# A list schedule, made in the source, sets the order of every engine of a hybrid encoder layer

## The chip, the cores and the metric

The kernel runs on one core of a Trainium2 chip. The core has TensorE (PE in the profile), VectorE (DVE), ScalarE (ACT), GpSimd (POOL) and SyncE (SP); each runs its own stream of instructions in order. SP issues nearly all transfers here, POOL a few. The metric is device microseconds of one execution.

## The reference

One layer of a streaming encoder, for 2048 prompt rows and for 8 running streams of 16 rows each that attend to 1024 cached rows. All matrices are float32.

```
h = rms_norm(x, norm_g)
z = einsum("btd,de->bte", h, w_in)                 # 1024 -> 3584 columns
u_a, v_a, g_a, q, k, v, g_b = split(z)             # 512 columns each
y_a = u_a * (tril(W_s) @ rms_norm(v_a) + b_s) * silu(g_a)      # in chunks of 128 rows
q, k = rms_norm(q), rms_norm(k)                    # per 64 columns
s = q @ k.T / 8 - slope * |distance|, masked by chunks of 64
o = (softmax(s_1) - lam * softmax(s_2)) @ v        # 4 heads, two halves each
y_b = rms_norm(o) * (1 - lam_init) * silu(g_b)
y = x + concat(y_a, y_b) @ w_out
```

The new keys, values and gate rows are outputs too.

## The kernel before, in words

Every float32 operand of a matmul is split into a high part, which ACT writes by a cast, and a low part, which DVE or POOL writes by a subtraction (`split`); a product is then two or three matmuls (`mm3`). Projection, the values of the prompt and the output projection take three.

The work is written as generators, each step of which emits a few instructions and yields its time on TensorE:

- Input projection and branch A (`stream` in `p1_pools`): 14 blocks of weight columns for the first 8 prompt tiles and the sample tile, then 14 for the other 8 tiles. A block's weights come in eight chunks (`load_w`: transfer to `wraw`, ACT and DVE split them into `w`); two row tiles share one accumulator (`acc`). Tiles of x are transposed on TensorE (`x_tp`, to `xT`). `mix` is the spatial gate.
- Sample attention (`sample_scores`, `sample_values`): `sk_tp` transposes cached keys, `sS` are scores, `sO` the products with values. Values come by SP into two buffers `svraw`, then ACT and POOL split them into two buffers `sv`.
- Prompt attention (`attention`): per head and pair of query tiles, `k_tp` and `q_tp` transpose keys and queries, `S` are scores, `a_tp` transposes of the probabilities, `oT` products with values, `o_tp` the transposes of a finished pair. Stage A does rows 0 to 1023 beside the second half of the projection, stage B the other rows beside the output projection.
- Output projection (`out_stream`): `y_tp` transposes rows of y (cast to `yT`), `oo` multiplies them by `wo`, the split `w_out`, whose raw chunks come into `woraw`.

`weave(a, b, ratio, ahead)` puts two generators together: it emits steps of `b`, and between them as many steps of `a` as `ratio` asks for. With `tc.issue_after` it also ties each step of `a` to a TensorE instruction of `b` some `ahead` steps back, so that `a` doesn't run too far ahead. The tile framework then orders the instructions of each engine: an instruction written earlier comes first, unless by the framework's own estimate of times it isn't ready and a later one is. SBUF pools lie over one another: when stage A's pools close, `wo` takes the space of the right side, and stage B's attention that of the projection on the left side.

## Time and profile before

| what | value |
|---|---|
| median of 3 runs | 1415.4 us (1412.22 to 1416.99) |
| span of the profiled execution | 1410.9 us |
| time of the profiled execution beyond its span | not in the page |
| TensorE busy | 1360.5 us, 96% |
| VectorE, ScalarE, GpSimd busy | 897.1, 794.0, 617.6 us |
| bytes moved | 183.06 MB, mean 130 GB/s |

Busy time of TensorE is the time in which at least one matmul is in flight. A window row shows, for a stretch of the span, each engine's busy time and instruction count, then TensorE's granted clock, the share of the 16 transfer engines in use, and GB/s. A wait row reads: engine, tile and line that waited, what released it, us in total, times, longest.

### The profile page before, as it was taken

What the parts mean: (1) busy time and instruction counts of PE and PEld (TensorE: products, weight loads), DVE (VectorE), ACT (ScalarE), POOL (GpSimd) and SP (SyncE); (2) the same over time, 40 slices, a digit from 0 to 9 for tenths busy, and PEclk for the clock granted to TensorE, in tenths of its full rate; (3) what the DMA queues carried; (4) which work ended last, traced back from release to release, by engine and by line L of the source; (5) the groups of instructions that cost most, each with busy time, mean ns of one, the idle gap of its engine ahead of it and who ended that gap; (6) DMA issues with size and microseconds to landing.
All of it is one profiled execution on the core that took longest, in us unless ns stands there. A gap on an engine that the chain in (4) does not pass through costs nothing.

```text
span 1410.9 us, 27990 instructions
## 1 busy us (share of the span) xinstructions
PE 1360.5 (96%) x9892; PEld 1266.1 (90%) x9892; DVE 897.1 (64%) x2114; ACT 794.0 (56%) x1778; POOL 617.6 (44%) x796
## 2 busy tenths in 40 slices
PE   7999999999999989899999999988999999999998
PEld 6999999999999979899999999986888888888887
DVE  5442366767565764786766767444888778878632
ACT  5442356666655775565554655443777767667520
POOL 2361535555554655656232331243555545444310
PEclk9999999999999999999999999998999999999999
DMA  7533244545444476445343332166555433433223
GB/s 220 175 91 100 78 122 124 169 130 158 130 140 145 142 220 203 112 112 138 96 128 83 99 96 69 42 211 207 149 158 162 142 115 117 143 97 94 75 94 101
DMA packets 209245, 183.06 MB, mean 130 GB/s; under 512 B 21104, under 2 KB 167024, under 8 KB 209104
## 3 DMA queue, kind: packets, MB, share of 16 engines
q1 hardware_dynamic: 199280, 155.17, 36.9%
q0 software_dynamic: 9824, 26.09, 6.8%
q8 instruction: 78, 1.28, 0.4%
q14 instruction: 63, 0.52, 0.1%
HBM read 130.86 MB, written 42.47 MB: 123 GB/s over the span
## 4 chain that ended last, share of the span: by engine, by line
PE 50%; DMA 7%; DVE 5%; ACT 3%; issue 3%; POOL 3%; SPq 1%; ACTq 0%; DVEq 0%; POOLq 0%
PE acc L73 16%; PE oo L73 12%; PE S L73 8%; PE oT L73 7%; PE a_tp L77 4%; DMA wraw<-in_w_in_dram 2%; DMA svraw<-in_cache_v_dram 1%; DMA woraw<-in_w_out_dram 1%; DVE ex L584 1%; DMA x<-in_x_prompt_dram 1%; DVE ex L568 1%; PE y_tp L77 1%; DMA qraw<-q_scr 1%; POOL sv L139 1%; DVE w L306 1%
## 5 line engine op out<-in xcount | busy, mean ns | idle before, releaser
L73 PE MATMUL acc<-w,xT 128*128 128x256 f32 x5376 | 719.4, 284 | 2.5 <-DVE w L306 0.9
L73 PEld LDWEIGHTS acc<-w,xT 128*128 128x128 f32 x5376 | 676.2, 190 | 14.8 <-issue 2.7
L73 PE MATMUL oo<-wo,yT 128*128 128x512 f32 x816 | 223.6, 405 | 6.6 <-ACT yT L138 6.6
L73 PE MATMUL S<-kT,qT 128*128 128x512 f32 (+3 forms) x688 | 185.8, 367 | 6.2 <-DVE sst L568 3.9
L572 ACT ACTIVATE ex<-ex,sst 128x128 f32<-128x128 f32 (+15 forms) x128 | 153.9, 1203 | 61.0 <-DVE sst L568 59.5
L73 PEld LDWEIGHTS oo<-wo,yT 128*128 128x128 f32 x816 | 148.9, 191 | 34.7 <-ACT yT L138 7.6
L306 DVE SCALAR_TENSOR_TENSOR w<-wraw,normg,w 128x256 fp32r<-128x256 f32 x224 | 119.6, 555 | 87.1 <-ACT w L305 79.1
L305 ACT ACTIVATE w<-wraw,normg 128x256 fp32r<-128x256 f32 x220 | 105.8, 505 | 87.8 <-DMA wraw<-in_w_in_dram 75.3
L73 PE MATMUL oT<-aT,v 128*128 128x256 f32 x864 | 151.8, 290 | 2.9 <-ACT aT L138 1.9
L568 DVE CUSTOM_DVE_ANT_0 ex<-S,dist,sst 128x512 f32<-128x512 f32 (+2 forms) x192 | 123.2, 652 | 37.6 <-PE S L73 35.8
L73 PEld LDWEIGHTS oT<-aT,v 128*128 128x128 f32 x864 | 124.3, 189 | 14.5 <-DVE aT L139 3.9
L139 POOL TENSOR_TENSOR sv<-svraw,sv 128x512 fp32r<-128x512 f32 (+1 forms) x72 | 96.6, 1346 | 75.5 <-ACT sv L138 59.1
L73 PEld LDWEIGHTS S<-kT,qT 128*128 128x128 f32 x688 | 110.4, 191 | 21.3 <-DVE sst L568 8.6
L138 ACT CAST aT<-a_tp 128x512 fp32r<-128x512 f32 (+1 forms) x144 | 79.3, 559 | 70.4 <-PE a_tp L77 68.5
L139 DVE TENSOR_TENSOR aT<-a_tp,aT 128x512 fp32r<-128x512 f32 (+1 forms) x144 | 94.3, 658 | 38.2 <-ACT aT L138 37.3
L568 DVE CUSTOM_DVE_ANT_0 ex<-S,dist 128x512 f32<-128x512 f32 (+3 forms) x128 | 79.6, 629 | 29.8 <-PE S L73 16.6
L77 PE MATMUL a_tp<-ident,ex 128*128 128x128 f32 x544 | 83.1, 273 | 4.3 <-DVE ex L584 3.3
L784 POOL TENSOR_TENSOR slo<-slo,dist_s 64x256 f32<-64x256 f32 (+1 forms) x64 | 49.4, 772 | 63.3 <-ACT slo L783 60.5
L139 POOL TENSOR_TENSOR v<-vraw,v 128x512 fp32r<-128x512 f32 x36 | 48.2, 1338 | 54.5 <-ACT v L138 45.4
L77 PEld LDWEIGHTS a_tp<-ident,ex 128*128 128x128 f32 x544 | 63.3, 140 | 8.5 <-DVE gbt L641 1.9
L584 DVE SCALAR_TENSOR_TENSOR ex<-ex,sst 128x1024 f32<-128x1024 f32 (+4 forms) x64 | 65.1, 1038 | 1.1
L588 POOL TENSOR_TENSOR ex<-ex 128x1024 f32<-128x1024 f32 (+4 forms) x32 | 58.4, 1848 | 15.9 <-ACT ex L587 11.4
(144 smaller groups left out, 1925.5 us busy)
## 6 DMA issues: line engine op xcount, KB each, us to landing
wraw<-in_w_in_dram SPq DMA_DIRECT2D x160, 128.0 KB, 2.5
skraw<-in_cache_k_dram SPq DMA_DIRECT2D x64, 256.0 KB, 3.1
svraw<-in_cache_v_dram SPq DMA_DIRECT2D x64, 256.0 KB, 2.9
kT<-k_scr POOLq DMA_DIRECT2D x20, 512.0 KB, 4.6
vraw<-out_dram SPq DMA_DIRECT2D x36, 256.0 KB, 2.8
y<-y_scr SPq DMA_DIRECT2D x34, 256.0 KB, 3.0
out_dram<-xo SPq DMA_DIRECT2D x34, 256.0 KB, 2.1
wraw<-in_w_in_dram SPq DMA_DIRECT2D x128, 64.0 KB, 2.2
```

Source lines behind the costliest of these rows:

```text
L73: pe.last = nc.tensor.matmul(*a, **k).ins
L77: pe.last = nc.tensor.transpose(*a, **k).ins
L138: act.copy(hi, src)
L139: (lo_eng or dve).tensor_tensor(out=lo, in0=src, in1=f(hi), op=ALU.subtract)
L305: act.activation(w[:, 0], r, AF.Copy, scale=normg[:, kc:kc + 1])
L306: dve.scalar_tensor_tensor(out=w[:, 1], in0=r, scalar=normg[:, kc:kc + 1], in1=f(w[:, 0]), op0=ALU.mult, op1=ALU.subtract)
L568: dve.tensor_tensor_reduce(out=ex[c][:, a:b], in0=s, in1=dist[:, off + a:off + b], scale=SLOPES[h], scalar=prev[c], op0=ALU.add, op1=ALU.m ...
L572: act.activation(ex[c][:, :w], ex[c][:, :w], AF.Exp, bias=prev[c], scale=-1.0, accum_out=st[:, c, 6:7])
L584: dve.scalar_tensor_tensor(out=p0, in0=p1, scalar=st[:, 1, 7:8], in1=p0, op0=ALU.mult, op1=ALU.add)
L588: pool.tensor_tensor(out=p0, in0=p1, in1=p0, op=ALU.add)
L784: pool.tensor_tensor(out=lo, in0=lo, in1=dist_s[rh, x:x + w_], op=ALU.add)
```

## The change

The order of all instructions is set in the source. When the whole program is written, and before the framework orders it, `Order(tc).run()` goes through the instruction list. It finds what each instruction must wait for from the memory that it reads and writes, which buffer of its tag each tile can take, and which tiles of a later pool lie over those of an earlier one. Then it plays a list schedule: each engine takes, whenever it is free, the first in program order of the instructions that are ready by then. Durations come from a table in `cost`; a transfer takes 1500 ns and its bytes at 280 per ns through one shared channel. An instruction on TensorE counts as ready only 150 ns (`SLACK`) after its producer on another engine has reached it, and one that waits for a transfer 150 ns (`LOAD`) after. The resulting order of each engine, SP and POOL with their transfers included, is handed to the framework as a chain of dependencies. In `weave` the tie with `tc.issue_after` is gone; the ratios and buffer counts are the same. The operations, their sizes, their buffers and the engine of each are the same; only comments are taken out besides, so a line n of the kernel before stands at about n + 288 in the code that follows the new class (L73 and L77 are now L361 and L365).

```diff
+class Order:
+    SLACK, LOAD = 150.0, 150.0
...
+    def cost(self, n):
+        kind = type(n.ins).__name__[4:]
+        size = max([math.prod([k for s, k in a.ap[1:]]) for a in n.reads + n.writes] or [1])
+        accum = len(n.writes) > 1
+        if n.dma:
+            return 0.0, 560.0 if n.engine == self.POOL else 400.0
+        if n.engine == self.PE:
+            size = math.prod([k for s, k in n.writes[0].ap[1:]])
+            t = 109.0 if size <= P else 4 + 0.4455 * size
+            return t + 165, t
+        if n.engine == self.ACT:
+            t = 165 + 0.83 * size if kind == "TensorCopy" else 205 + 0.835 * size
+            return (t + 180, t + 90) if accum else (t, t - 105)
+        if n.engine == self.DVE:
+            t = {"TensorTensor": 160 + 1.04 * size, "TensorReduce": 160 + 1.03 * size, "Memset": 100 + 0.5 * size,
+                 "Reciprocal": 162.0}.get(kind, 205 + 1.04 * size)
+            if kind == "TensorScalarPtr" and not n.ins.is_scalar_tensor_tensor:
+                t = 170 + 0.56 * size
+            return (t + 100, t - 40) if accum else (t, t - 85)
+        if kind == "Memset":
+            return 100 + 0.83 * size, 100 + 0.83 * size
+        if "pow" in str(n.ins):
+            return 300 + 200.0 * size, 250 + 200.0 * size
+        t = 190 + 2.16 * size if kind == "TensorTensor" else 195 + 1.1 * size
+        return t, t - 50
+    def run(self):
+        N = self.nodes
+        reach = {self.PE: 54.0, self.POOL: 80.0, self.SP: 27.0}
+        for n in N:
+            n.wait = len(n.deps)
+            for d in n.deps:
+                N[d].after.append(n.idx)
+        first = [[] for _ in N]
+        gate = [[] for _ in N]
+        def behind(a, b):
+            first[a].append(b)
+            N[b].wait += 1
+        for q in self.queue.values():
+            for a, b in zip(q, q[1:]):
+                if self.uses[a][0] != self.uses[b][0]:
+                    behind(self.uses[a][0], self.uses[b][0])
+        for name in self.tag:
+            u = self.uses[name]
+            N[u[0]].new.append(name)
+            for b in u[1:]:
+                if u[0] not in N[b].deps:
+                    behind(u[0], b)
+        for g in self.gates:
+            for i in g[1]:
+                gate[i].append(g)
+            for i in g[2]:
+                N[i].wait += 1
+        cost = [self.cost(n) for n in N]
+        ready = [0.0] * len(N)
+        left = {k: len(q) for k, q in self.queue.items()}
+        users = {x: len(self.uses[x]) for x in self.tag}
+        last, slot, taken, freed = {}, {}, set(), {}
+        free = {n.engine: 0.0 for n in N}
+        later, now_, held = {e: [] for e in free}, {e: [] for e in free}, set()
+        out = {e: [] for e in free}
+        dma = 0.0
...
+        for n in N:
+            if not n.wait:
+                arrive(n.idx)
+        while place():
+            pass
+        for _ in N:
+            t, _, e = min((free[e] if now_[e] else max(free[e], later[e][0][0]), e.value if hasattr(e, "value") else str(e), e)
+                          for e in free if now_[e] or later[e])
+            while later[e] and later[e][0][0] <= t:
+                heapq.heappush(now_[e], heapq.heappop(later[e])[1])
+            i = heapq.heappop(now_[e])
+            n = N[i]
+            out[e].append(i)
+            if n.dma:
+                size = 4 * math.prod([k for s, k in n.writes[0].ap])
+                dma = max(t + 1500, dma) + max(size / 280, 60.0)
+                end = dma + 200
+            else:
+                end = t + cost[i][0]
+            free[e] = t + cost[i][1]
+            for j in n.after:
+                b = N[j].engine
+                if b == e and not n.dma and not N[j].dma:
+                    r = free[e]
+                else:
+                    r = end + reach.get(b, 35.0) + (self.SLACK if b == self.PE else 0) + (self.LOAD if n.dma else 0)
+                ready[j] = max(ready[j], r)
+                N[j].wait -= 1
+                if not N[j].wait:
+                    arrive(j)
+            more = list(first[i])
+            for g in gate[i]:
+                g[0] -= 1
+                if not g[0]:
+                    more += g[2]
+            for j in more:
+                ready[j] = max(ready[j], t)
+                N[j].wait -= 1
+                if not N[j].wait:
+                    arrive(j)
+            for name in n.tiles:
+                if name in users:
+                    last[name] = max(last.get(name, 0.0), end + 35)
+                    users[name] -= 1
+                    if not users[name]:
+                        taken.discard(slot[name])
+                        freed[slot[name]] = last[name]
+            while held and place():
+                pass
+        info = mybir.DependencyInfo(mybir.DependencyClass.NoSync, mybir.DependencyReason.DATA)
+        for q in out.values():
+            for a, b in zip(q, q[1:]):
+                self.tc.add_manual_dep(N[b].ins, N[a].ins.name, info, reason="order")
...
     def weave(a, b, ratio, ahead):
         x = y = 0.0
-        marks = []
         for cost in b:
             if cost is None:
                 return
             y += cost
-            if cost:
-                marks.append(pe.last)
             while x < y * ratio:
-                with tc.issue_after(marks[-1 - ahead]) if len(marks) > ahead else nullcontext():
-                    cost = next(a, None)
+                cost = next(a, None)
...
+    Order(tc).run()
```

Three places show what moves.

SP, where the last loads of w_out stand (`woraw`; `wraw` are projection weights, `vo` and `ya` results of the projection's blocks, `xo` rows of x for the output projection). Before:

```order
L940 DMA woraw_11486<-in_w_out_dram 128x1024
L363 DMA out_3_dram<-vo_13080 128x2x256
L419 DMA y_scr12_80<-ya_13087 128x128
L419 DMA y_scr13_81<-ya_13087 128x128
L419 DMA y_scr14_82<-ya_13087 128x128
L419 DMA y_scr15_83<-ya_13087 128x128
L940 DMA woraw_11492<-in_w_out_dram 128x1024
L978 DMA xo_13253<-in_x_sample_dram 128x512
L940 DMA woraw_11498<-in_w_out_dram 128x1024
```

Now:

```order
L1224 DMA woraw_11492<-in_w_out_dram 128x1024
L585 DMA wraw_12026<-in_w_in_dram 128x128
L586 DMA wraw_12026<-in_w_in_dram 128x128
L1224 DMA woraw_11498<-in_w_out_dram 128x1024
L585 DMA wraw_12035<-in_w_in_dram 128x128
L586 DMA wraw_12035<-in_w_in_dram 128x128
L585 DMA wraw_12044<-in_w_in_dram 128x128
```

Before, six of the eight loads came after the last weight load, between the last blocks' stores. Now all stand between weight loads, and the weights of three more blocks and a part of a fourth follow the last of them.

TensorE, the end of stage A's attention (`o_tp` is its last finished pair). Before:

```order
L73 MATMUL oT<-aT,v 128x256 x5
L73 MATMUL acc<-w,xT 128x256 x24
L77 MATMUL o_tp<-ident,os 128x128 x2
L73 MATMUL acc<-w,xT 128x256 x35
L73 MATMUL mix<-vhl,wsT 128x512 x3
L73 MATMUL acc<-w,xT 128x256 x96
```

Now:

```order
L361 MATMUL oT<-aT,v 128x256 x5
L361 MATMUL acc<-w,xT 128x256 x7
L365 MATMUL o_tp<-ident,os 128x128 x2
L361 MATMUL acc<-w,xT 128x256 x99
L361 MATMUL mix<-vhl,wsT 128x512 x3
L361 MATMUL acc<-w,xT 128x256 x96
```

From here to the first `oo` stood 227 acc, and now stand 1059; from the first `S` to here stood 2248, and now 1235. In both orders `y_tp` and the first `oo` follow the last acc directly. The first `q_tp` of stage B stood 6 oo ahead of its first `S` and now 15.

TensorE, values of the last sample batch (`sO`; two for each key tile `sv`). Before:

```order
L73 MATMUL sO_7408<-sv_7440,saT_7364 128x512
L73 MATMUL sO_7408<-sv_7480,saT_7364 128x512
L73 MATMUL acc_7391<-w_6859,xT_7082 128x256 x2
L73 MATMUL sO_7408<-sv_7480,saT_7364 128x512
L77 MATMUL x_tp_7106<-ident_98,x_6975 128x128 x4
L73 MATMUL acc_7391<-w_6859,xT_7082 128x256
```

Now:

```order
L361 MATMUL sO_7408<-sv_7480,saT_7364 128x512
L361 MATMUL acc_7489<-w_7448,xT_6557 128x256 x3
L361 MATMUL acc_7489<-w_7456,xT_6557 128x256 x3
L361 MATMUL acc_7489<-w_7464,xT_6557 128x256 x3
L361 MATMUL acc_7571<-w_7278,xT_6646 128x256
L361 MATMUL sO_7408<-sv_7506,saT_7364 128x512
```

Before, products of two key tiles could stand together, with transposes of x and q between them; now acc alone stands there, 14 to 32 between the first products of two key tiles.

## The prediction

> **What bounds the kernel now.** First the head of the page: TensorE is busy nearly all the time.

> ```profile
> span 1410.9 us, 27990 instructions
> PE 1360.5 (96%) x9892; PEld 1266.1 (90%) x9892; DVE 897.1 (64%) x2114; ACT 794.0 (56%) x1778; POOL 617.6 (44%) x796
> ```

> No other engine is above 64%. But 96% busy is not 96% streaming, since a short run of matmuls counts its pipeline latency as busy. So I price each matmul by its spacing in long unbroken runs, and compare stage by stage. The price rows are a stretch in which PE does only projection, a run of 512-wide matmuls, a group of transposes, and three groups of the page.

> ```profile
> 50.00:100.00 50.00, 50.00 (x425) 50.00 (x424) 21.32 (x37) 20.52 (x42) 27.31 (x26) 1.00 0.39 112
> ...
> 1380.51 7.94 PE L73 MATMUL oo<-wo,yT 128*128 128x512 f32 x33
> 1388.29 1.04 PE L77 MATMUL y_tp<-ident,y 128*128 128x128 f32 x8
> ...
> 29.14 0.60 PE L77 MATMUL x_tp<-ident,x 128*128 128x128 f32 x4
> 29.50 3.39 PE L73 MATMUL acc<-w,xT 128*128 128x256 f32 x24
> ...
> L73 PE MATMUL acc<-w,xT 128*128 128x256 f32 x5376 | 719.4, 284 | 2.5 <-DVE w L306 0.9
> L73 PE MATMUL oo<-wo,yT 128*128 128x512 f32 x816 | 223.6, 405 | 6.6 <-ACT yT L138 6.6
> L73 PE MATMUL S<-kT,qT 128*128 128x512 f32 (+3 forms) x688 | 185.8, 367 | 6.2 <-DVE sst L568 3.9
> ```

> 256 columns: 50 / 425 = 0.1176 us. 512 columns: (1388.29 - 1380.51) / 33 = 0.235. A transpose: (29.50 - 29.14) / 4 = 0.09. A score matmul S mixes widths: its mean of 367 ns lies 83/121 of the way from 284 to 405, so 0.1176 + 0.69 x 0.117 = 0.20.

> Then all engines by stage (engines in the order PE, PEld, DVE, ACT, POOL, with instruction counts), and after it PE's counts alone: acc in three stages, transposes (line 77) in four, oo in two, oT in one, S in three.

> ```profile
> 0.00:50.00 50.00, 39.69 (x301) 38.02 (x302) 27.11 (x84) 27.20 (x54) 11.66 (x29) 1.00 0.71 220
> 50.00:200.00 150.00, 150.00 (x1276) 150.00 (x1275) 60.20 (x111) 57.23 (x123) 66.42 (x68) 1.00 0.35 100
> 200.00:500.00 300.00, 295.34 (x2338) 282.77 (x2337) 203.60 (x463) 193.93 (x484) 160.48 (x184) 1.00 0.48 145
> 500.00:600.00 100.00, 91.16 (x665) 82.74 (x664) 60.46 (x132) 60.46 (x136) 58.61 (x69) 0.98 0.59 173
> 600.00:900.00 300.00, 297.65 (x2421) 292.76 (x2421) 209.95 (x526) 165.12 (x453) 105.27 (x185) 1.00 0.37 101
> 900.00:1000.00 100.00, 86.91 (x549) 77.16 (x549) 47.74 (x100) 44.62 (x94) 40.63 (x50) 0.93 0.57 170
> 1000.00:1350.00 350.00, 342.93 (x2058) 295.46 (x2057) 271.86 (x678) 236.09 (x418) 172.65 (x208) 1.00 0.42 123
> ```

> ```profile
> 0.00:50.00 50.00, 32.89 (x228) 1.00 0.71 220
> 500.00:600.00 100.00, 70.16 (x507) 0.98 0.59 173
> 900.00:1000.00 100.00, 39.08 (x317) 0.93 0.57 170
> ...
> 0.00:50.00 50.00, 12.42 (x73) 1.00 0.71 220
> 500.00:600.00 100.00, 11.88 (x72) 0.98 0.59 173
> 900.00:1000.00 100.00, 9.02 (x55) 0.93 0.57 170
> 1000.00:1350.00 350.00, 80.77 (x525) 1.00 0.42 123
> ...
> 900.00:1000.00 100.00, 27.48 (x90) 0.93 0.57 170
> 1000.00:1350.00 350.00, 149.37 (x538) 1.00 0.42 123
> ...
> 1000.00:1350.00 350.00, 97.37 (x564) 1.00 0.42 123
> ...
> 500.00:600.00 100.00, 7.95 (x34) 0.98 0.59 173
> 900.00:1000.00 100.00, 14.64 (x50) 0.93 0.57 170
> 1000.00:1350.00 350.00, 118.80 (x431) 1.00 0.42 123
> ```

> What each stage loses against pure streaming:
> - 0 to 50 us: 228 x 0.1176 + 73 x 0.09 = 33.4, so 16.6 lost.
> - 500 to 600 (end of the sample batches, start of prompt attention): 507 x 0.1176 + 34 x 0.2 + 72 x 0.09 + 52 others at the middle of 256 and 512 columns, 0.176, = 82.1, so 17.9 lost.
> - 900 to 1000 (projection ends, output projection starts): 317 x 0.1176 + 90 x 0.235 + 50 x 0.2 + 55 x 0.09 + 37 others, mostly oT, x 0.135 = 78.4, so 21.6 lost.
> - 1000 to 1350: 564 x 0.1176 + 538 x 0.235 + 431 x 0.2 + 525 x 0.09 = 326.3, so 23.7 lost.
> - By the same prices 0.8 is lost in 50 to 200, 17.7 in 200 to 500, 4.5 in 600 to 900 and 5.2 in the last 61 us.

> Together 107 us of 1410.9; the rest, about 1303, no order of instructions can remove. The third reading is what PE waits for, over the whole run:

> ```profile
> PE x_tp L77 <- DVE x L262: 7.5, 1, 7.5
> PE oo L73 <- ACT yT L138: 6.6, 3, 5.3
> PE q_tp L77 <- DMA qraw<-q_scr: 4.1, 2, 3.3
> ...
> PE S L73 <- DVE qT L142: 2.1, 1, 2.1
> ```

> These are single gaps at seams, not a steady shortage. The page's idle of PE is about 50 us; the other 57 hide in stretched "busy" time.

> **The change part by part.** No arithmetic, buffer or transfer is added; only each engine's order and the order of the transfer queues move. So the sum is: what of the 107 us goes, and what is put in elsewhere.

> *Start.* The 7.5 us wait for the first normalized tile stays: the first transfers are the same. Of the other 9.1, eight transposes now stand together per tile and two token tiles are fetched ahead of two weight chunks, which helps one side and delays the other. I take -2.6 (bounds 0 and -5).

> *Sample batches, 200 to 500.* The rows are moved finely, without a place that I can price singly. Half of 17.7 is my value: -8.7, with bounds 0 and -14 (the loss rate of 600 to 900, 4.5 per 300, would leave about 4).

> *End of the sample batches.* Before, values sO of two key tiles stand together or two acc apart, with x tiles, mixes and first keys between; each key tile waits for POOL's split:

> ```profile
> L139 POOL TENSOR_TENSOR sv<-svraw,sv 128x512 fp32r<-128x512 f32 (+1 forms) x72 | 96.6, 1346 | 75.5 <-ACT sv L138 59.1
> ```

> In the new order only acc stand between, 14 to 32 a key tile, 1.6 us and more against POOL's 1.35, and the x tiles are done earlier. I take 17.9 down to 7.5: -10.4 (bounds -3 and -14). What covers it is the projection's acc. If a transfer into svraw is late, PE now stands with nothing taken past it.

> *Prompt attention of the first half.* This is where it can get worse. Before, first S to last o_tp contains 2248 acc; now 1235, and 1059 acc follow as a plain tail where 227 did. The stretch before:

> ```profile
> 543.00:913.00 370.00, 363.85 (x2946) 356.31 (x2946) 249.75 (x620) 199.13 (x543) 141.03 (x230) 1.00 0.37 101
> ```

> Its projection part of DVE is 2248 x (60.2 / 1236 acc of 50 to 200) = 109 us, so attention is 140. The same attention now stands beside 1235 acc (60 us of DVE) in about 237 us of streaming (1235 + 240 oT at 0.1176, 208 S at 0.2, the rest transposes): DVE at 84%, where it was 67%. In 1000 to 1350 DVE was at 78% and PE lost 6.8%. At that rate 237 us lose 16, against about 10 lost in the 370 before (by the same prices 360 of them stream): +6 (bounds 0 and +19). The tail loses nothing, as 50 to 200 shows.

> *Seam to the output projection.* The loads of w_out now stand among the weight loads, behind the attention's last store and ahead of most of the tail, not behind it. Before, PE stood 5.3 us:

> ```profile
> 945.79 1.14 ACT L138 CAST wo<-woraw 128x512 fp32r<-128x512 f32 x2 [2.98 <-DMA woraw<-in_w_out_dram]
> ...
> 947.95 2.07 PE L73 MATMUL oo<-wo,yT 128*128 128x512 f32 x4 [5.31 <-ACT yT L138]
> ```

> The first yT cast was queued on ACT behind that wo cast, which waited for a transfer, so the reason goes. Next late is the short chain y_tp, ACT's cast, about 0.57 us by half of that row, since oo follows y_tp at once: about 1.5 us stays. The four oo after the gap took 2.07 us, 0.5 each for 0.235, and the granted clock was 0.93 over this stage, so 7 of the 21.6 us are clock, which falls with the gaps. The 3.3 us for qraw and 2.1 us for qT came behind it: the first queries' transposes stood 6 oo (1.4 us) ahead of the first scores, the second ones 3 oo behind those; now 15 oo (3.5 us) lie between, and the second come behind all scores of the first pair. I leave 2 us of the two. 21.6 to 8.6: -13 (bounds -6 and -18).

> [...]

> *Prompt attention of the second half.* Counted along PE, oo, S and oT stand nearly where they stood; what moves is a few places at a time. I take 23.7 to 16: -7.8 (bounds +5 and -18). The end: 0, the last 48 oo and two stores are the same.

> Sum: -2.6 - 8.7 - 10.4 + 6 - 13 - 7.8 = -36.5, a span of 1374.4. The page gives no time for this execution beyond its span; the median of the runs, 1415.4, is 4.5 above the span. That makes **1379 us**.

> **The rivals.** *All seams close (1350).* The change's cost table is close to the rows: 190 + 2.16 x 512 = 1296 ns for POOL's 512-wide subtraction, 1346 in the row above. If the dense stretch then costs nothing and every other term sits near its better bound, -65: 1350. Against it: transfers, whose landing varies, are ordered in one queue.

> *Order too tight: slower (1440).* PE takes nothing past a late instruction, and the planner leaves it only 150 ns behind its producer. What it prices as uncontended need not be:

> ```profile
> L139 DVE TENSOR_TENSOR wo<-woraw,wo x8: 679/1354/1378, 920.9 to 947.0; 128x512 fp32r<-128x512 f32 x8
> L139 POOL TENSOR_TENSOR wo<-woraw,wo x8: 1265/1294/1347, 922.2 to 946.5; 128x512 fp32r<-128x512 f32 x8
> ```

> The DVE split of w_out takes 0.68 us alone and 1.35 beside POOL's, 0.67 later. In the dense stretch some 104 score groups (208 S, two each) and 40 value groups hang on DVE; a mean lateness of 0.45 us, two thirds of that, costs PE 144 x 0.45 = 65 instead of the +6: -36.5 + 59 = +22, so 1438, about 1440. It decides from 0.3 us on (42 / 144), where the gain is gone. [...]

> [...]

> *The gain is eaten, no change (1412).* Same place, a mean lateness of 0.28 us: 40 for the 6, so -2. *The order is not what it says* is excluded: the listed order differs on every engine.

> **How the numbers follow.** Forecast, 1360 to 1398, 0.55; all seams close, 0.20; eaten, 1398 to 1420, 0.12; slower, 0.13. A measurement here tells a change from about 0.3%, 4 us: faster is 0.55 + 0.20 + about half of 0.12 = 0.81; same 0.05; slower 0.14. The terms' bounds sum to 1346 and 1430; the range 1345 to 1413 leaves out the slower rival and the edge of the third.

> **What would show it.** The gap of 5.3 us before the first oo is under 2 us, the clock there near 1.0, the last woraw lands over 60 us before the first oo; first S to last o_tp takes about 250 us with DVE above 80%, with a tail of 1059 acc at 0.118 each; 500 to 600 loses under 10. Wrong if PE's waits for DVE in the dense stretch grow past 20 us, or if sO waits for POOL or a transfer again.

## The result: 1452.6 us, slower by 2.7%

The changed kernel takes 1452.57 us (median of 4 runs, 1447.43 to 1456.06), the kernel before, run beside it, 1414.35 (1412.22 to 1416.99). The ratio is 1.027, with a 95% interval of 1.023 to 1.030. The forecast was 1379, in a range of 1345 to 1413: the sign is wrong, and the time lies beyond even the 1430 to which the prediction's worse bounds summed.

The head of the page of the changed kernel, span and engines:

```profile
span 1445.3 us, 27962 instructions
PE 1372.6 (95%) x9892; PEld 1258.0 (87%) x9892; DVE 904.9 (63%) x2114; ACT 797.0 (55%) x1778; POOL 630.1 (44%) x796
```

The span grew by 34.4 us, PE's busy time by 12.1 and its idle time from 50.4 to 72.7 (1410.9 - 1360.5 and 1445.3 - 1372.6): PE waits more, and some of the rest is again stretched "busy" time. What PE waits for over the whole run (engine, tile and line, releaser: us in all, times, longest):

```profile
PE x_tp L365 <- DVE x L550: 10.4, 4, 8.8
PE a_tp L365 <- DVE gbt L929: 6.5, 10, 1.2
PE sO L361 <- POOL sv L427: 6.4, 10, 1.6
PE acc L361 <- DVE xT L427: 3.2, 1, 3.2
PE sO L361 <- ACT sv L426: 3.0, 6, 0.9
```

The seams of before (oo behind yT 5.3 us, q_tp behind qraw 3.3) are gone from the top. In their place stand many short waits, about 0.65 us each in the rows of a_tp and sO (6.5 / 10, 6.4 / 10), right behind a producer. Engines by stage in the changed kernel (columns as in the prediction: window, length, then PE, PEld, DVE, ACT, POOL, and the clock), and behind them the rows of before for the sample stage and for the attention of the first half:

```profile
198.50:595.60 397.10, 372.39 (x2879) 349.54 (x2877) 244.34 (x538) 242.92 (x579) 198.28 (x227) 1.00 0.49 144
595.60:852.90 257.30, 244.75 (x1921) 234.44 (x1920) 204.31 (x521) 156.27 (x420) 116.15 (x191) 1.00 0.41 109
852.90:987.20 134.30, 132.16 (x1082) 129.91 (x1080) 54.72 (x107) 47.34 (x140) 34.80 (x52) 1.00 0.37 110
```

```profile
191.30:543.40 352.10, 342.40 (x2662) 324.00 (x2660) 231.75 (x517) 228.01 (x551) 187.07 (x215) 1.00 0.51 155
543.40:913.80 370.40, 364.25 (x2951) 356.76 (x2950) 249.95 (x620) 199.40 (x543) 140.94 (x232) 1.00 0.37 101
```

The sample stage runs from the first sk_tp to the first S. Its PE idle time went from 9.7 us to 24.7 (397.10 - 372.39).

**The ledger.** The two orders put different numbers of acc into a stage, so lengths can't be compared, but losses can: length less streaming, at the prediction's prices, with sS as 256 columns, sO as 512 and mix at 0.206. For the changed sample stage: 2036 acc and 256 sS at 0.1176, 144 sO at 0.235, 1 S at 0.2, 36 mix at 0.206 and 406 transposes at 0.09 make 347.5, and 397.1 - 347.5 = 49.6. The four stages meet at the same piece of work in every kernel. Worked out so for the two kernels and for those of the first row of experiments below (us lost):

| stage | before | the change | list order from the sample batches on | from stage A's attention on | from the w_out loads on | from stage B on | no order, no tie |
|---|---|---|---|---|---|---|---|
| start to first sk_tp | 17.2 | 28.1 | 19.9 | 16.8 | 18.0 | 18.1 | 18.2 |
| first sk_tp to first S | 30.4 | 49.6 | 49.6 | 38.1 | 28.5 | 30.9 | 31.5 |
| first S to first oo | 16.4 | 26.7 | 27.2 | 25.0 | 64.0 | 16.4 | 13.7 |
| first oo to last oo | 41.5 | 35.6 | 34.9 | 36.2 | 38.0 | 40.3 | 87.1 |
| sum | 105.5 | 140.0 | 131.6 | 116.1 | 148.5 | 105.7 | 150.5 |

In the change +10.9, +19.2 and +10.3 us ahead of the first oo, and -5.9 behind it. The streaming is the same, 1301.6.

One profile stands behind each column, so a cell has scatter. Up to the first oo the kernel before, "from stage B on", "no order, no tie" and a later one (50 / 0 from stage B on, below) have the same order on every engine; their sample stages lose 30.4, 30.9, 31.5 and about 35, the last with fewer idle us of PE (9.4) than the first (9.7), at a granted clock of 0.98 in that stage instead of 1.00. A difference of 4 or 5 us in one cell can be that.

### The profile page after: what moved, and what is told of

It is laid out like the page before. It is cut to its first block, busy times and chain, and to the rows that moved or that the text cites. A ratio compares the mean times of both kernels' runs of the same rounds, so it can differ in the third digit from the quotient of the medians.

```text
span 1445.3 us, 27962 instructions
## 1 busy us (share of the span) xinstructions
PE 1372.6 (95%) x9892; PEld 1258.0 (87%) x9892; DVE 904.9 (63%) x2114; ACT 797.0 (55%) x1778; POOL 630.1 (44%) x796
## 4 chain that ended last, share of the span: by engine, by line
PE 63%; DMA 10%; DVE 9%; ACT 6%; issue 6%; POOL 4%; SPq 2%; DVEq 0%; ACTq 0%; POOLq 0%
PE acc L361 30%; PE oo L361 10%; PE S L361 7%; PE oT L361 6%; PE a_tp L365 4%; DMA x<-in_x_prompt_dram 3%; DMA wraw<-in_w_in_dram 2%; ACT ex L860 2%; DVE ex L856 2%; PE sS L361 2%; PE sk_tp L365 1%; DVE w L594 1%; PE sO L361 1%; DVE ex L872 1%; DMA skraw<-in_cache_k_dram 1%
## 5 line engine op out<-in xcount | busy, mean ns | idle before, releaser
L361 PE MATMUL acc<-w,xT 128*128 128x256 f32 x5376 | 718.6, 284 | 8.6 <-DVE xT L427 3.2
L361 PEld LDWEIGHTS acc<-w,xT 128*128 128x128 f32 x5376 | 676.8, 190 | 23.6 <-DVE w L594 4.5
L361 PE MATMUL oo<-wo,yT 128*128 128x512 f32 x816 | 236.7, 402 | 0.8 <-ACT yT L426 0.8
L361 PE MATMUL S<-kT,qT 128*128 128x512 f32 (+3 forms) x688 | 187.8, 363 | 7.1 <-DMA qT<-qT 2.7
L361 PEld LDWEIGHTS oo<-wo,yT 128*128 128x128 f32 x816 | 145.3, 188 | 24.1 <-ACT yT L426 1.0
L361 PE MATMUL oT<-aT,v 128*128 128x256 f32 x864 | 153.3, 294 | 1.3 <-ACT aT L426 1.3
L361 PEld LDWEIGHTS S<-kT,qT 128*128 128x128 f32 x688 | 111.2, 189 | 24.5 <-DVE sst L856 8.6
L361 PEld LDWEIGHTS oT<-aT,v 128*128 128x128 f32 x864 | 122.0, 189 | 11.6 <-ACT aT L426 4.9
L365 PE MATMUL a_tp<-ident,ex 128*128 128x128 f32 x544 | 91.3, 278 | 11.7 <-DVE gbt L929 6.5
L365 PEld LDWEIGHTS a_tp<-ident,ex 128*128 128x128 f32 x544 | 63.0, 140 | 34.2 <-DVE gbt L929 13.2
L426 ACT CAST sv<-svraw 128x512 fp32r<-128x512 f32 (+1 forms) x72 | 44.4, 616 | 39.1 <-PE sO L361 19.7
```

The lines of the kernel that those rows point to most:

```text
L361: pe.last = nc.tensor.matmul(*a, **k).ins
L365: pe.last = nc.tensor.transpose(*a, **k).ins
L426: act.copy(hi, src)
```

## The experiments

**Where it is lost: the order imposed from later and later on.** In four kernels the list schedule is made as in the change, but only instructions emitted from a certain place on are chained in its order; what is ahead of the place is left to the framework, with the tie of the weaves that the change removed. The edit, here with the mark at stage A's attention:

```diff
         for q in out.values():
+            q = [i for i in q if i >= FROM[0]]
             for a, b in zip(q, q[1:]):
...
+        FROM[0] = sum(type(i).__name__ != 'BassTilePoolBoundary' for i in tc.nc.cur_bb.bb.instructions)
         att = attention_a()
```

The mark ahead of the first sample batch:

> The list order is imposed only from the first sample batch on; the start (0 to about 190 us) is left to the framework as before, and the ties of the weaves are off as in the change. Theory 'each stage pays for its own tight order': the loss that the change adds up to the first sk_tp (+10.8 us) goes, the rest stays: 1441 us (1436 to 1446). Rival 'one plan, cut in two': instructions behind the cut were planned for other arrival times, so the sample stage loses more and the time stays above 1448.

1438.87 us (1438.6 to 1440.03), ratio 1.0175 (1.0147 to 1.0203). The time falls by 13.7, of which the ledger shows 8.2 in the start (the change's runs lie up to 9 us apart, and its profiled one is the quickest of the four); the sample stage loses the change's 49.6. The rival falls.

The mark at stage A's attention:

> The list order is imposed only from the first half's prompt attention on; start and sample batches are as before, tie included. Theory 'each stage pays for its own': the +10.8 of the start and the +19.2 of the sample batches go: 1422 us (1416 to 1428), and the stretch from first S to first oo still loses about 10 us more than before. Rival 'lateness is carried over' (the dense stretch pays only because the sample stage left transfers late): that stretch loses what it lost before, and the time is 1405 to 1413.

1423.61 us (1419.63 to 1429.41), ratio 1.0073 (1.0042 to 1.0104). Another 15.3 us come back. The attention from first S to first oo still loses 25.0, so the loss is its own and not lateness that it inherits. The first S came at 573.1 us instead of 543.4, and the sample stage loses 7.7 more than before. By the same prices 6.2 us are lost between 543.0 and 573.1, where the first keys and queries now stand in the list order.

The mark at stage B:

> The list schedule's order is imposed from the first instruction of stage B on alone; before that the framework orders, with weave's tie. By the two traces the stretch from the first output projection to the end lost 44.0 us before and 39.7 with the change, and its seam lost 5.6 and 6.6 beside a longer tail: this gives 1405 to 1412 if the stages are independent. If the gain there came from what stage A left behind (w_out split early), it is 1412 to 1420.

1411.54 us (9 runs, 1410.0 to 1416.36), ratio 0.9981 (0.9964 to 0.9998). In the second half the list order loses as little as the tied weave that it replaces (40.3 against 41.5). It is the best kernel of this study, by a difference below the 0.3% that the prediction took as the limit of telling.

And the mark at the loads of w_out, which should have taken the seam's gain alone:

> The list order is imposed only from the loads of w_out on (tail of the projection, seam, second half); everything ahead of them is as before. Theory: the gap before the first oo goes from 5.3 us to under 2 and the second half runs as in the run that imposed the order from there on (about 458 us from first oo to the end): 1408 us (1404 to 1412). Rival 'the gap is hidden elsewhere': the time equals that run's, 1411 to 1414, though the gap is shorter.

1456.0 us (1454.5 to 1458.76), ratio 1.0297 (1.0266 to 1.0327): 48 us above the 1408 of the theory and at least 42 above the rival's range. The seam did close (1.2 us from the last acc to the first oo), but first S to first oo lost 64.0. The transfer queue of that kernel (start, us, engine line, op, tiles, count):

```profile
848.63 14.67 SPq L935 DMA_DIRECT2D y_scr<-gbt  x4
863.34 0.90 SPq L1252 DMA_DIRECT2D y<-y_scr  x2
864.34 2.62 SPq L1233 DMA_DIRECT2D woraw<-in_w_out_dram  x2
870.42 0.38 SPq L587 DMA_DIRECT2D wraw<-in_w_in_dram  x1
```

The w_out loads wait for the end of the attention, and the weight loads of the tail are chained behind them. So the tail can't be run ahead any more: from first S to last o_tp stood 1515 acc instead of 2248, with 960 left behind it instead of 227. That the attention, in the framework's order, had too little to fill its gaps is the likely reading; PE stood idle for 36.5 us of the stage instead of 11.5. With the mark at this place the seam's 5 us cost 48 in the same stage. Whether another place would do better stays open.

**What the lost tie is worth.** The change made, but its schedule not imposed:

```diff
-    Order(tc).run()
+    pass
```

> The changed kernel without the list schedule: only the tie of weave is gone, the framework orders the engines as before. Theory 'the list schedule is too tight' (each instruction stands where exact durations would have it, so lateness falls on the engines in order): the framework's own order stays loose, so this is near the kernel before, 1405 to 1425 us. Rival 'the lost tie' (one stream runs ahead of the other without it, whoever orders the engines): this is as slow as the changed kernel, 1440 to 1460.

1457.7 us (1454.02 to 1458.38), ratio 1.0299 (1.0256 to 1.0342), the figure of the lost tie. But all of it lies in the second half, 87.1 us lost instead of 41.5. Up to the first oo the framework put every engine in the very order of the kernel before, tie or no tie (63.4 against 64.0 us lost), and it is there that the change loses. The like times of this kernel and the change have different causes. So the change consists of two things: it takes away a tie that is worth some 46 us in the second half (87.1 - 41.5), and puts a list order there that is worth 51.5 (87.1 - 35.6). The stages ahead of it, where the tie changed nothing, have only the list order's own cost, 40 us (104.4 - 64.0).

**The start: an engine that stands in order.** DVE of the changed kernel, with what ended the idle time before each row, and PE beside it:

```profile
17.21 0.75 DVE L550 TENSOR_SCALAR x<-x,xst 128x1024 f32<-128x1024 f32 x1
21.65 0.23 DVE L410 TENSOR_SCALAR subg<-subg 128x128 f32<-128x128 f32 x1 [3.69 <-DMA subg<-in_subln_g_dram]
24.05 0.22 DVE L415 CUSTOM_DVE_ANT_0 keep<-keep 128x64 f32<-128x64 f32 x1 [2.18 <-DMA keep<-in_lambda_k_dram]
24.20 0.08 DVE L415 DVE_READ_ACCUMULATOR2_ANT lame<- 128x1 f32 x1
24.20 1.28 DVE L427 TENSOR_TENSOR xT<-x_tp,xT 128x512 fp32r<-128x512 f32 x2
```

```profile
18.93 2.84 PE L361 MATMUL acc<-w,xT 128*128 128x256 f32 x22
24.94 0.74 PE L361 MATMUL acc<-w,xT 128*128 128x256 f32 x4 [3.18 <-DVE xT L427]
```

Constants that nothing needs yet (subg, lambda) are placed by the table where it has them land. They land later (subg a measured 2.9 us after issue and lambda's k rows 5.5, where the table, without a queue, has 1.9 and 1.8), DVE stands, and the xT splits behind them make PE stand 3.18 us. The kernel before has the same chain, shorter: the framework too puts the constants ahead of an xT split (DVE, then PE).

```profile
31.09 0.23 DVE L122 TENSOR_SCALAR subg<-subg 128x128 f32<-128x128 f32 x1 [2.52 <-DMA subg<-in_subln_g_dram]
32.58 0.23 DVE L127 CUSTOM_DVE_ANT_0 keep<-keep 128x64 f32<-128x64 f32 x1 [1.26 <-DMA keep<-in_lambda_k_dram]
```

```profile
34.18 0.66 PE L77 MATMUL x_tp<-ident,x 128*128 128x128 f32 x4 [1.29 <-DVE xT L139]
```

So the list order's own part of the 3.18 is some 1.9 us. POOL does the like at the very first tile, before and in the change:

```profile
5.11 0.19 POOL L259 TENSOR_TENSOR xst<-xst 128x1 f32<-128x1 f32 x1 [3.41 <-ACT xsq L257]
```

```profile
6.14 0.48 POOL L590 TENSOR_SCALAR w<-wraw,normg 128x256 fp32r<-128x256 f32 x1 [4.44 <-DMA wraw<-in_w_in_dram]
6.59 0.19 POOL L547 TENSOR_TENSOR xst<-xst 128x1 f32<-128x1 f32 x1
```

The small step of the first tile's norm (xst) stood ahead of the first weight split, and now waits behind it for the weights to land. The first transpose of x starts at 8.8 us instead of 7.5.

With SP and POOL released:

```diff
-        for q in out.values():
+        for e_, q in out.items():
+            if e_ not in (self.PE, self.ACT, self.DVE):
+                continue
             for a, b in zip(q, q[1:]):
```

> The list order is imposed on PE, ACT and DVE alone; SP and POOL take what the framework gives them. Theory 'PE's place just behind its producers is what costs': the loss stays, 1440 to 1465 us, and the waits of sO and x_tp stay. Rival 'the queue order is what costs' (constants ahead of tiles at the start, loads behind waiting loads): at least half of the 40 us that the change loses by the first oo goes, under 1432 us.

1460.51 us (1457.5 to 1462.44), ratio 1.0324 (1.0287 to 1.0361): imposing the order of the transfer queues isn't what costs. The start even shows the mechanism enlarged, since SP now issues subg at 23.59 us instead of 18.69, while DVE still waits for it in its place (SP of the change, then SP, DVE and PE of this kernel):

```profile
18.69 0.43 SPq L409 DMA_DIRECT2D subg<-in_subln_g_dram  x1
```

```profile
23.59 0.47 SPq L411 DMA_DIRECT2D subg<-in_subln_g_dram  x1
```

```profile
27.93 0.23 DVE L412 TENSOR_SCALAR subg<-subg 128x128 f32<-128x128 f32 x1 [10.16 <-DMA subg<-in_subln_g_dram]
...
29.50 1.28 DVE L429 TENSOR_TENSOR xT<-x_tp,xT 128x512 fp32r<-128x512 f32 x2
```

```profile
30.24 1.22 PE L363 MATMUL acc<-w,xT 128*128 128x256 f32 x4 [8.64 <-DVE xT L429]
```

Then the constants' steps moved back, by planning their loads (`LATE` names lambda, subln and slope) to land 12 us late:

```diff
                 end = dma + 200
+                if any(k in n.reads[0].bass_ap.tensor.name for k in LATE):
+                    end += 12000
```

> The change, but the planner takes the loads of lambda, subln and slope to land 12 us later than its table says, so their small DVE steps (L410 and L415 of the profile) stand behind the next xT splits. Loads, arithmetic and everything else stay. Theory 'DVE stands in order at a late constant and holds the xT behind it': PE's gap of 3.18 us at 24.94 us goes, the loss up to the first sk_tp falls from 28 us to 22 to 25, and the time from 1452.5 to 1445 to 1450. Rival 'the constants cost by their place in the transfer queue': the gap stays, 1450 to 1455.

1447.48 us (1446.62 to 1449.89), ratio 1.0253 (1.0229 to 1.0277). The time is as expected, but it can't be told from the change's (1447.43 to 1456.06), and the ledger's start fell only from 28.1 to 26.6. The 3.18 us are gone, and the next late thing has their place, now on ACT (of this kernel):

```profile
25.13 1.06 ACT L550 ACTIVATE xsq<-x 128x1024 bf16<-128x1024 f32 x1 [4.41 <-DMA x<-in_x_prompt_dram]
...
26.18 1.05 ACT L431 CAST xT<-x_tp 128x512 fp32r<-128x512 f32 x2
```

That x tile was issued behind a row of constants on SP. So in another kernel, without the 12 us, the loads themselves were held back to 36 us of the planner's time (`LATE` has the gate's bias and two masks besides):

```diff
         ready = [0.0] * len(N)
+        for n in N:
+            if n.dma and any(k in n.reads[0].bass_ap.tensor.name for k in LATE):
+                ready[n.idx] = 36000.0
```

> The change, but the planner may issue the loads of lambda, subln, slope, the gate's bias and its two masks only from 36 us of its own time on; on SP the x tiles then stand ahead of them, and so do the xT splits on DVE. Theory 'the start loses by constants, on SP ahead of the x tiles and on DVE ahead of the splits': the loss up to the first sk_tp falls from 28 us to 19 to 22, near the 19.9 of the run with a free start, and the time to 1440 to 1445. Rival 'the x tiles are late for another reason' (their slots come free late, since eight transposes stand together per tile): the loss stays at 25 us or more and the time at 1446 or above.

1448.64 us (1446.14 to 1450.64), ratio 1.0238 (1.0213 to 1.0263). The first 50 us now lose 18.8 (before 16.6, the change 22.1), but from there to the first sk_tp 8.2 are lost where before lost 0.6 and the change 6.0, so the start as a whole stays at 27.0. Constants in front of splits are shown as the cause of the 3.18 us; they are not shown as the cause of the start's 11 us, which stays open. Each mended lateness let the next one through: in that kernel 2.1 us for the sample rows' xTs and 1.9 for sq_tp behind a transfer.

**The sample stage: how much is lateness.** PE's waits there, before and in the change:

```profile
PE sO L73 <- POOL sv L139: 1.5, 3, 0.8
...
PE sO L73 <- ACT sv L138: 1.3, 3, 0.5
```

```profile
PE sO L361 <- POOL sv L427: 6.4, 10, 1.6
PE sO L361 <- ACT sv L426: 3.0, 6, 0.9
PE sk_tp L365 <- DMA skraw<-in_cache_k_dram: 2.5, 3, 1.0
PE mix L361 <- DVE xT L427: 2.3, 2, 1.2
PE mix L361 <- ACT vhl L426: 2.3, 2, 1.5
```

15 of the stage's 19 us are idle time of PE, most of it in front of these: sO is placed behind its split by the table's time and 150 ns. The splits themselves became no slower: POOL's 128x512 sv takes 1335 ns on average (1336 before), and the values land a median of 2.9 us after issue in both kernels. More room was tried in four kernels, by the planner's two constants (SLACK behind any producer of PE, LOAD behind a transfer). LOAD alone:

```diff
-    SLACK, LOAD = 150.0, 150.0
+    SLACK, LOAD = 150.0, 1500.0
```

> The changed kernel with LOAD 1500 ns for 150: what waits for a transfer is planned 1.35 us later, all else as it was. Theory 'transfers land later than planned' (x tiles 5.2 us for 3.6 planned, small constants 4.7 for 1.8): the loss of the start and the sample batches mostly goes, 1410 to 1425. Rival 'too tight between engines': the waits for POOL and ACT stay, 1440 to 1455.

Both, SLACK 1000 and LOAD 1500:

> SLACK 1000 for 150 and LOAD 1500 for 150: TensorE's instructions are planned 0.85 us further behind their producers too. Theory 'too tight': 1385 to 1410, below the kernel before. Theory 'transfers alone': as with LOAD alone within 5 us. Rival 'lost tie' or 'the planned order is bad in itself': 1440 or more.

These two up to stage B only, 150 and 150 behind it:

> The change with SLACK 1000 and LOAD 1500 for everything that is emitted ahead of the second half's attention, and 150 and 150 behind it. The losses add up theory: up to the first oo as in the run with both raised everywhere (976.8 us for the first oo), from there on as in the change (453 us): 1432 us (1428 to 1437). Rival 'what one stage gains the next gives back': the second half loses the 9 us again, as where both were raised everywhere: 1440 to 1445.

The same with SLACK 3000:

> As the run with SLACK 1000 and LOAD 1500 ahead of the second half, but SLACK 3000 there. Theory 'the rest is lateness as well': the loss of the sample batches falls from 40 us to 32 to 35, and the time from 1434 to 1426 to 1430. Rival 'a floor: beyond the usual delay, more slack only makes the plan keep work waiting for slots and piles up transposes': the sample batches stay at 38 us or more and the time at 1431 or above.

| kernel | time (range), ratio (interval) | start | sample stage | first S to first oo | second half |
|---|---|---|---|---|---|
| the change, 150 / 150 | 1452.57 (1447.43 to 1456.06), 1.0266 (1.0232 to 1.0300) | 28.1 | 49.6 | 26.7 | 35.6 |
| 150 / 1500 | 1452.57 (1451.88 to 1457.07), 1.0279 (1.0234 to 1.0324) | 31.0 | 48.2 | 20.8 | 44.8 |
| 1000 / 1500 | 1442.16 (1441.75 to 1444.48), 1.0201 (1.0161 to 1.0240) | 28.5 | 42.3 | 21.7 | 41.8 |
| 1000 / 1500 up to B | 1433.9 (1432.25 to 1436.72), 1.0161 (1.0132 to 1.0189) | 27.7 | 39.7 | 20.6 | 36.7 |
| 3000 / 1500 up to B | 1456.5 (1455.89 to 1462.09), 1.0332 (1.0303 to 1.0360) | 32.1 | 42.6 | 44.0 | 36.2 |

Losses add up by stage: the third row's front and the change's second half make the fourth, 1432 expected and 1433.9 measured. It is the best order of the list schedule over the whole kernel that was tried, 19 us better than the change and 21 worse than before. LOAD alone changes nothing in the time, and both together stay 32 us above the 1385 to 1410 that "too tight" had promised. SLACK 1000 takes most of the waits of sO away (9.4 us to 2.8); others come up, and at 3000 others again (waits of PE in the sample stage, of the fourth and of the fifth kernel):

```profile
PE x_tp L369 <- DVE xT L431: 8.1, 6, 2.5
...
PE sO L365 <- POOL sv L431: 1.3, 5, 0.5
```

```profile
PE sk_tp L369 <- DVE skT L431: 9.6, 10, 2.0
```

So 7 to 10 of the 19 us are lateness that slack buys back (the third and fourth kernels have the same order in this stage, so the 2.6 between them is scatter). Beyond that is a floor near 40: the theory that all of it is lateness falls, and at 3000 stage A pays for the room (44.0). What makes up the other 9 to 12 stays open.

In the second half it goes the other way: with LOAD 1500 it loses 9 us more, with both raised 6. Is tighter still better there? The kernel with the mark at stage B, with this edit besides:

```diff
-    SLACK, LOAD = 150.0, 150.0
+    SLACK, LOAD = 50.0, 0.0
```

> The list order from the second half's attention on, as in the run that took 1411.5 us, but with SLACK 50 and LOAD 0 in place of 150 and 150; all ahead of it as before, tie included. Theory 'in the second half slots, not lateness, limit, so a tighter plan is the better one' (losses there: 35.6 us at 150/150, 44.8 with LOAD 1500, 41.8 with both raised): 1405 to 1410. Rival 'too tight there as well below 150': 1413 to 1420, with longer waits of PE for DVE.

1414.89 us (12 runs, 1409.84 to 1418.91), ratio 1.0019 (1.0002 to 1.0035). The second half loses 42.7 instead of 40.3, with a longer wait of PE for DVE (with 150 / 150, then with 50 / 0):

```profile
PE a_tp L369 <- DVE ex L876: 3.8, 4, 1.2
```

```profile
PE a_tp L369 <- DVE ex L876: 5.8, 5, 2.1
```

The theory falls: tighter is not better. The time is where the rival had it, and the wait grew as it said, by 2 us. But the two profiled spans differ by 4.5 us, of which some 4 lie in the sample stage, where both kernels have the same order. So that below 150 the second half is too tight is not shown. Why room behind transfers costs it 6 to 9 us, where it costs the first half nothing, stays open.

**One engine's order alone.** Only PE chained (the edit of the queues' experiment with other engines named), and only ACT and DVE:

> Only PE keeps the list order; ACT, DVE, POOL and SP take what the framework gives them. Theory 'the other engines, held in order, are late for PE' (as DVE at the start): the loss up to the first oo falls by half or more of the 40 us, sample batches under 40 us lost, time under 1435. Rival 'PE's own order, each matmul close behind its producer, is what costs': the sample batches still lose 46 to 52 us, time 1445 to 1465.

> Only ACT and DVE keep the list order; PE, POOL and SP take what the framework gives them, without the tie of the weaves, which by itself costs 45 us in the second half. Theory 'ACT and DVE in order are late for PE': the start loses 25 us or more and the sample batches 40 or more, where the run without any imposed order lost 18 and 31. Rival 'PE's own order costs': start and sample batches within 4 us of 18 and 31.

PE alone: 1503.14 us (1501.83 to 1510.24), ratio 1.0658 (1.0618 to 1.0698); 26.0 lost in the start, 68.9 in the sample stage, 40.9 and 67.3 behind. ACT and DVE alone: 1597.52 us (1595.98 to 1599.02), ratio 1.1313 (1.1282 to 1.1344); 30.7, 87.1, 61.9 and 112.0. Both are worse in the sample stage than all engines together (49.6) and than none (31.5). PE alone lies beyond both of its expectations. ACT and DVE alone meets the numbers of its theory (25 or more, 40 or more), but loses so much more than the change in each stage that it can't tell which engine's order costs the change. What the two show is that the orders are cut to each other: some engines held to a plan that the others don't keep wait more than all that keep it.

## Why the prediction was wrong, step by step

By the ledger, whose stages nearly match the terms, the forecast of the span missed by 71 us (-36.5 against +34.4): 38 in the sample batches and their end, 16 in the seam and the second half together, 13.5 in the start, 3.5 in the dense stretch.

**The start (-2.6 foreseen, +10.9 measured).** The step that failed was "the first transfers are the same". SP's first ten issues are, to 5.6 us; from there constants stand ahead of x tiles, and what stands behind a late transfer on POOL, DVE and ACT is other work than before. The queue behind a waiting instruction was counted for PE and not for the others. The bounds, 0 and -5, left out a loss altogether. Of the 10.9 us, 5.5 fall into the 50 us that the term was about (16.6 to 22.1); 5.4 fall into the stretch from there to the first sk_tp, for which the sum has no term, and their cause stays open.

**The sample batches and their end (-8.7 and -10.4 foreseen, +19.2 measured).** This is the main failure. The step was "Half of 17.7 is my value", and for the end "17.9 down to 7.5": a part that could not be priced singly was taken to improve because it moves, on the loss rate of a stage in which another order already streamed. The pricing of the end compared the 1.6 us between the products of two key tiles with POOL's 1.35 and found it enough, and POOL's price was right (1335 ns measured). But sO waited 6.4 us for POOL and 3.0 for ACT all the same: what counts is when the split can start, and a plan that leaves 150 ns puts the product right behind where it expects the split to end. Room behind the producers bought 7 to 10 us of the 19 back; the rest stays open. Waits of sO for POOL were named as a sign of being wrong, and they came (1.5 us before).

**The dense stretch (+6 foreseen, +9.5 measured).** Right in sign and nearly in size: 257 us long (about 250 foreseen), DVE at 204.31 / 257.30 = 79% (84 foreseen), 20.1 lost instead of 10.6. The mechanism, DVE's load, is not what the waits show: PE's waits for DVE went from 4.7 to 6.7 us, those for transfers from 0.8 to 3.1 and those for ACT from 0.5 to 2.2. So the size is in part luck. The tail behind it, "loses nothing" in the prediction, lost 5.6 up to the last acc.

**The seam (-13 foreseen).** The gap is as described; the last w_out cast began at 883.0 us, 105 ahead of the first oo:

```profile
L426 ACT CAST wo<-woraw x16: 604/619/642, 854.6 to 883.0; 128x512 fp32r<-128x512 f32 x16
```

```profile
988.20 0.98 PE L361 MATMUL oo<-wo,yT 128*128 128x512 f32 x3 [0.77 <-ACT yT L426]
...
989.37 2.77 PE L361 MATMUL oo<-wo,yT 128*128 128x512 f32 x11
```

5.31 became 0.77, and the next 11 oo take 0.25 each, at a granted clock of 1.00 (988.2 to 992.2 us). That is right. The 13 foreseen counts most of the 7 us of clock as gone, with a gap of 1.5 us still there; that such a gap costs no clock, no row beside the sum shows. The change bears it out: in the 5 us behind each of its seven gaps of 1.47 to 1.75 us (the longest ends at 544.28) the clock was 1.00 too. **The second half (-7.8 foreseen):** the waits for qraw and the clock of the first oo lie behind the first oo, so the ledger's -5.9 is to be held against some 9 of the seam's 13 (all but the gap's 3.8) and these 7.8 together: the sign was right, the size a third. The gain the seam gave up front was eaten by the tail's 5.6.

**The rivals.** "Order too tight: slower" had a mechanism that is at work, 150 ns and no way past a late instruction, and came within 13 us of the time, at a chance of 0.13. Slack bought back 19 of the 38 us, so about half of the loss is shown to be tightness. Its place was wrong: it was looked for only in the dense stretch, which cost 3.5 us more than forecast, while the stages that the forecast credited with 22 us of gain paid 30. The prediction also priced the list order only. That the same diff takes away the weaves' tie, worth some 46 us in the second half, stands nowhere in its sum; the list order had to earn that much in the second half before it gained anything.

## What to carry to other kernels

A static order is worth no more than its arrival times: before crediting a scheduler with the idle time of an old order, ask of every engine, not only the bottleneck, what it puts behind an instruction whose data comes by transfer. Loss that a trace shows as stretched busy time belongs to no wait and should be given no sign until one is found. A change that replaces an old rule and adds a new one is two changes: price both, and impose the new order stage by stage, since here it was neutral to useful in the last third and cost 40 us ahead of it.

## What the runs showed of the hardware that was not expected

```profile
24.90:26.40 1.50, 0.85 (x5) 0.67 (x6) 1.50 (x3) 0.95 (x1) 0.00 (x0) 0.97 0.52 146
26.40:27.90 1.50, 1.50 (x9) 1.50 (x9) 0.53 (x2) 1.16 (x4) 0.84 (x2) 0.50 0.33 74
27.90:29.40 1.50, 1.50 (x9) 1.50 (x8) 0.37 (x3) 1.23 (x4) 0.00 (x0) 0.50 1.02 308
29.40:31.00 1.60, 1.60 (x14) 1.60 (x14) 1.60 (x3) 0.34 (x2) 0.00 (x0) 0.90 0.91 311
```

The clock stays at 1.00 for some 1.4 us after the long gap, is down to 0.50 when PE comes back from the short one at 26.29, and is up again some 3 us later; over these 6 us that adds some 1.7 to the gap's 3.2. Which of the two brought it down, the trace doesn't tell; behind the change's gaps of 1.47 to 1.75 us it stayed at 1.00. Behind the 8.64 us gap of the kernel with SP and POOL released it was 0.50 at once:

```profile
30.20:33.20 3.00, 2.84 (x13) 2.58 (x13) 2.84 (x7) 0.49 (x1) 0.00 (x0) 0.50 0.57 164
```

In the first 40 us a load of 0.2 KB took as long to land as one of 128 KB (tiles, queue, count, KB each, median us from issue to landing, in the changed kernel):

```profile
wraw<-in_w_in_dram SPq DMA_DIRECT2D x19, 128.0 KB, 4.9
...
bias_s<-in_sgu_b_dram SPq DMA_DIRECT2D x8, 0.2 KB, 4.7
...
keep<-in_lambda_k_dram SPq DMA_DIRECT2D x2, 32.0 KB, 5.5
```

Over the whole run the 128 KB loads of wraw took a median of 2.6. The change's table has 0.06 us of transfer and 1.7 around it for the 0.2 KB, and 0.1 us for the 32 KB: 3 to 4 us too early in these 40 us, in which 0.68 of the transfer engines is in use (0.34 from 50 to 200 us), and the lambda loads are among those behind which DVE stood.
